# State-space rounds: a new order of ScalarE's copies, with gate products ahead of one transpose

## The chip, the cores and the metric

The kernel runs on one core of one Trainium2 chip. The metric is the device time of one execution in microseconds (us); lower is better.

## The reference

A decoder trunk of two layers over one sequence of 512 tokens with 1024 channels, in float32. Layer 0 mixes tokens with a state-space model, layer 1 with attention; each is followed by a gated convolutional feed-forward layer, and each part is modulated by a shift, a scale and a gate made from a conditioning vector (adaLN). The change touches the state-space mixer alone:

```python
def s5_mixer(h, w_in, lam_re, lam_im, log_dt, b_re, b_im, c_re, c_im, d_skip, w_glu, w_out):
    u = h @ w_in                                   # 512 x 1024
    ug = u.reshape(Bsz, S, S5_GROUPS, S5_GROUP)    # 64 groups of 16 channels
    ...                                            # each group drives 64 complex states:
    # state[t] = lam_bar * state[t-1] + B_bar u[t]; y[t] = Re(C state[t])
    y = y + d_skip * u
    y = gelu(y)
    y = y * sigmoid(y @ w_glu)
    return y @ w_out
```

## The kernel before

Matrix products are made with three TensorE products for each pair of tiles: a float32 weight is copied by ScalarE into a rounded part `w_hi`, and another engine subtracts that to get the rest, `w_lo` (`parted` and `rested` do the two steps for the input weights, `gate_hi` and `gate_lo` for the gate's, `y_hi` and `y_lo` for the mixer's output y).

The state-space mixer runs in eight rounds, m = 0 to 7, in the text "round zero" to "round seven"; each finishes one tile of 128 channels (8 groups). The 512 tokens are cut into 64 blocks of 8. Within a block the output is a direct product with a small Toeplitz table `t`; between blocks the states are scanned on VectorE. The order of instructions is the order in which the program is written, for each engine by itself (TensorE, ScalarE, VectorE, GpSimd and SyncE, whose queue SP issues nearly all transfers); nothing is rearranged by a planner. One round m does, in this order:

- `s5_scan(m)`: TensorE brings the inputs into the states (L1062); VectorE rotates, scans along the blocks with the decay table `cf` (L1073 to L1084), and leaves the states `ua`.
- the adaLN row of an earlier round is summed on VectorE (`row_sum`, L265).
- `s5_columns(m + 1)` for the next tile: TensorE makes the tile's kernel (L1007, L1010), ScalarE copies it out (`ktt`, L1015), TensorE transposes the tile's states' weights (L1021), ScalarE copies those out (`w`, L1022), TensorE transposes the kernel (L1025), ScalarE copies that out (`kt`, L1026), and SP stores it in DRAM (`s_z`).
- `s5_shifted(m + 1)`: SP loads the kernel back in shifted copies (`tw`, one buffer); in a later step ScalarE makes the table `t` of it in eight instructions (L1040).
- `inputs(m + 2)`: 24 TensorE products with the input weights of tile m + 2 (L323), a ScalarE copy `uf` (L1320), a store, and then `turn_u` loads u back in another layout.
- `s5_outputs(m)`: TensorE products with `t` (L1094) and with the states (L1103), then the gelu on ScalarE (`yg`, L1109) and a store of y.
- `parted(m + 4)` on ScalarE, `s5_decay(m + 1)` (the table `cf`, L1047), and the second step of `s5_shifted(m + 1)`, the table `t`.
- `s5_made(m + 2)` and `s5_states_out(m + 1)`: products on VectorE (L976), each followed by a sum on GpSimd (L980). The first gives `x`, which `s5_columns` reads a round later.

Beside these, one or two steps of the adaLN product of the next part run in the first four rounds (`ada_step`, L1164; `ada_load` brings the weights of the step after next, 2 x 512 KB; `row` loads one adaLN row of 512 KB), and from round four on the gate's weights are loaded and split, y is read back (`read`), and the first gate products are made (`glu_in`, L1369; `HEAD` is 4, the number of gate tiles begun early). Of the input weights `load_w(m + 4)` is issued in round m; 512 KB each.

Numbers of buffers set other waits: three `raw` buffers for loaded weights, one for `tw`, one for `cf`, one for `x`, two for `t`, and four PSUM banks (`aux`) for all small products.

Of the kernel before, what the change touches and what calls it, by code (L numbers as in the profile page):

```python
# [19 lines left out]
KT = D // P  # L20
# [796 lines left out]
class S5(Trunk):  # L817
# [301 lines left out]
    def s5(self, i, nxt):  # L1119
        nc, tc = self.nc, self.tc  # L1120
        ud = self.dram.tile([KT, GM, CG, L, B], F32, name="s5_ud")
        self.yd = self.dram.tile([KT, GM, CG, L, B], F32, name="s5_yd")
        HEAD = 4
        full = slice(0, S)
        with ExitStack() as stack:
# [16 lines left out]
            def rested(m, e=nc.gpsimd):  # L1142
                src, hi = w[m]
                lo = self.rest([P, KT, P])
                e.tensor_tensor(lo, src, hi.bitcast(F32), ALU.subtract)
                w[m] = [(hi[:, k], lo[:, k]) for k in range(KT)]
# [28 lines left out]
            with ExitStack() as start:  # L1175
# [93 lines left out]
                def turn_u(m):  # L1269
                    us[m] = self.s5q.tile([P, GM, B], F32, name="u", bufs=3)  # L1270
                    nc.sync.dma_start(us[m], ud[m].rearrange("g c j b -> (c j) g b"))
# [43 lines left out]
            def inputs(m):  # L1315
                ps = self.mm.tile([P, S], F32, name="mmp")
                for k in range(KT):
                    self.mms(ps, w[m], split_x, k, KT, full)
                uf = self.tmp.tile([P, L, B], F32, name="uf", tag="nm_t")
                nc.scalar.activation(uf, ps.rearrange("p (b j) -> p j b", j=L), AF.Copy)  # L1320
                store_u(m, uf)

            def columns_in(m):
                if m > 1 and m + 1 < KT:
                    self.s5_diagonal(m + 1)
                cols[m] = self.s5_columns(m, xs.pop(m))
                ws[m] = next(cols[m])
# [17 lines left out]
            def y_hi(*ms):  # L1345
                for m in ms:
                    nc.scalar.activation(yhi[:, m], yt[m], AF.Copy)
# [5 lines left out]
            def gate_load(n):  # L1353
                raw[n] = self.raw([P, KT, P], self.io["s5_w_glu"][n])

            def gate_hi(*ns):
                for n in ns:
                    hi[n] = self.wpool.tile([P, KT, P], F32R, name="w_hi", bufs=WB)
                    nc.scalar.activation(hi[n], raw[n], AF.Copy)

            def gate_lo(e, *ns):
                for n in ns:
                    lo[n] = self.rest([P, KT, P])
                    e.tensor_tensor(lo[n], raw[n], hi[n].bitcast(F32), ALU.subtract)
# [21 lines left out]
            for m in range(KT):  # L1386
                more, last = m + 1 < KT, m == KT - 1
                sts[m] = self.s5_scan(m, ws.pop(m), us[m], cfs.pop(m))
                next(sts[m])
                if m % 2 == 0 and m + 2 < KT:  # L1390
                    self.s5_tables(slice(m * 4 + 8, m * 4 + 16), 3, 5)
                elif m % 2 and more:
                    self.s5_tables(slice(m * 4 + 4, m * 4 + 12), 5, 6)
                if m == 0:
                    parted(3)
                if m + 3 < KT:
                    rested(m + 3)
                if m == 0:
                    turn_u(1)
                sts[m] = next(sts[m])  # L1400
                if 0 < m < KT - 3:
                    row_sum()
                if m == KT - 3:
                    read(0, 1, 2, 3)
                    gate_lo(nc.gpsimd, 0)
                if m == 0:
                    ada_step()
                    inputs(2)
                if more:
                    columns_in(m + 1)  # L1410
                    next(cols[m + 1])
                if m == KT - 3:
                    gate_hi(1)
                    gate_lo(nc.gpsimd, 1)
                if 0 < m < 4:
                    ada_step()
                if m + 4 < KT:
                    load_w(m + 4)
                if m == KT - 4:
                    for n in range(3):  # L1420
                        gate_load(n)
                if m == KT - 3:
                    gate_load(3)
                    gate_load(HEAD)
                if more:
                    ts[m + 1] = self.s5_shifted(m + 1)
                    next(ts[m + 1])
                if m and m + 2 < KT:
                    inputs(m + 2)
                if m + 2 < KT:  # L1430
                    turn_u(m + 2)
                if m < KT - 4:
                    row()
                if m == KT - 3:
                    self.rooms, self.rests = WB, 3
                    yhi = self.normed("a_hi", WHOLE)
                    ylo = self.normed("a_lo", WHOLE)
                    y_hi(0, 1, 2, 3)
                if m == KT - 2:
                    gate_hi(2)  # L1440
                    y_hi(4)
                    gate_hi(3)
                    y_hi(5)
                    for n in range(3):
                        for k in range(4):
                            glu_in(k, n, 0)
                if last:
                    y_hi(6)
                    y_lo(nc.gpsimd, 6)
                    for k in range(4):  # L1450
                        glu_in(k, 3, 0)
                    for n in range(HEAD):
                        for k in range(4):
                            glu_in(k, n, 1)
                    for n in range(HEAD):
                        for k in range(4, 6):
                            for j in range(2):
                                glu_in(k, n, j)
                outs[m] = self.s5_outputs(m, us.pop(m), ts.pop(m))
                next(outs[m])  # L1460
                outs[m].send((w2s.pop(m), sts.pop(m)))
                if m + 4 < KT:
                    parted(m + 4)
                if m == KT - 4:
                    gate_hi(0)
                if m == KT - 2:
                    gate_hi(HEAD)
                if more:
                    cfs[m + 1] = self.s5_decay(m + 1)
                    ts[m + 1] = next(ts[m + 1])  # L1470
                if steps:
                    ada_step()
                if m + 2 < KT:
                    xs[m + 2] = self.s5_made(m + 2)
                if m == KT - 3:
                    for n in range(4):
                        y_lo(nc.gpsimd, n)
                    read(4, 5)
                    row()
                    row()  # L1480
                if more:
                    w2s[m + 1] = self.s5_states_out(m + 1)
                if m == KT - 2:
                    y_lo(nc.gpsimd, 4, 5)
                    read(6)
# [378 lines left out]
```

## Time and profile before

| What | Value |
|---|---|
| Runs before | 1196.79, 1197.05, 1198.26 us (median 1197.05) |
| Profiled execution | 1199.56 us |
| Its span, first to last instruction | 1197.8 us |
| TensorE busy | 1159.5 us (97%) |
| VectorE busy | 942.5 us (79%) |
| ScalarE busy | 649.1 us (54%) |
| GpSimd busy | 204.8 us (17%) |
| Mean granted TensorE clock | 0.991 |

In the profile PE is TensorE's products, PEld its weight loads, DVE VectorE, ACT ScalarE, POOL GpSimd, and SP or SPq the queue that issues transfers. "L1025" is line 1025 of the kernel. A row of the timeline gives start, duration, engine, line, operation, what is written and read, and in brackets how long the engine stood idle before it and what ended that. The view of transfers gives the size of one and the time from its issue to its landing. The state-space rounds lie between about 50 and 180 us of the span; the text calls the engines by either name.

### The profile page before, as it was taken

Reading aid. Unit: us, or ns where it says so; the run is one execution under the profiler, and the core shown is the slowest. Engines: PE = TensorE matmul, PEld = TensorE weight load, DVE = VectorE, ACT = ScalarE, POOL = GpSimd, SP = SyncE. Lnnn points to the kernel's source line nnn. Section 1 sums busy time; section 2 is a strip of 40 time slices with the busy share of each in tenths; the row PEclk is TensorE's granted clock in tenths of the full one; section 3 lists DMA queues with packets and bytes.
Section 4 is the critical chain, followed back from the end, with each engine's and each line's share of the span. In section 5 each row is a group of like instructions: output and inputs, shape, how many; then the busy total and the mean of one; then the engine's idle time right before and its main releaser. Section 6 shows DMA issues by size and latency. Waiting matters only on the chain.

```text
span 1197.8 us, 21400 instructions
## 1 busy us (share of the span) xinstructions
PE 1159.5 (97%) x8255; PEld 1032.8 (86%) x8255; DVE 942.5 (79%) x1724; ACT 649.1 (54%) x1169; POOL 204.8 (17%) x268
## 2 busy tenths in 40 slices
PE   7987899999999999999999999999999999999997
PEld 2565788899999999989899788878999899999987
DVE  8957665879888788877676788876899878888855
ACT  3643554436666666666543576654457455555543
POOL 5664650000011111111000443330000000000000
PEclk9989899999999999999999999999999999999999
DMA  9777657833698898898704654623122332332331
GB/s 354 249 249 263 197 159 265 298 123 102 165 258 240 223 263 225 226 248 222 193 30 135 218 184 154 207 81 95 49 89 94 111 125 87 111 124 92 106 88 72
DMA packets 80006, 202.74 MB, mean 169 GB/s; under 512 B 23983, under 2 KB 26767, under 8 KB 78879
## 3 DMA queue, kind: packets, MB, share of 16 engines
q1 hardware_dynamic: 73423, 181.96, 45.2%
q0 software_dynamic: 6192, 18.88, 9.0%
q8 instruction: 65, 1.06, 0.4%
q10 hardware_dynamic: 288, 0.52, 0.1%
q14 instruction: 38, 0.31, 0.1%
HBM read 194.41 MB, written 6.92 MB: 168 GB/s over the span
## 4 chain that ended last, share of the span: by engine, by line
PE 77%; DVE 8%; DMA 7%; ACT 4%; issue 2%; POOL 1%; SPq 0%; DVEq 0%; ACTq 0%; POOLq 0%
PE mmp L323 41%; PE mmp L583 15%; PE aux L583 6%; PE mmp L1605 3%; DMA raw<-in_w_up 3%; PE aux L1751 2%; DVE w_lo L307 2%; PE aux L1734 1%; DMA raw<-in_s_w_in 1%; DVE sums L554 1%; ACT t L1040 1%; PE mmp L1369 1%; DVE ada_raw L265 1%; PE mmp L1378 1%; PE aux L1704 1%
## 5 line engine op out<-in xcount | busy, mean ns | idle before, releaser
L302 ACT ACTIVATE w_hi<-raw 128x1024 fp32r<-128x1024 f32 (+4 forms) x196 | 171.9, 887 | 114.0 <-PE mmp L323 55.1
L307 DVE TENSOR_TENSOR w_lo<-raw,w_hi 128x1024 fp32r<-128x1024 f32 (+4 forms) x153 | 154.1, 1011 | 31.6 <-ACT w_hi L302 27.8
L323 PE MATMUL mmp<-ghi,w_hi 128*128 128x512 f32 (+1 forms) x392 | 144.1, 368 | 0.0
L323 PE MATMUL mmp<-glo,w_hi 128*128 128x512 f32 (+1 forms) x392 | 143.7, 367 | 0.0
L323 PE MATMUL mmp<-ghi,w_lo 128*128 128x512 f32 (+1 forms) x392 | 143.6, 366 | 0.0
L323 PE MATMUL mmp<-a_hi,w_hi 128*128 128x256 f32 (+1 forms) x440 | 140.9, 323 | 0.0
L323 PE MATMUL mmp<-a_hi,w_lo 128*128 128x256 f32 (+1 forms) x440 | 139.0, 317 | 0.0
L323 PE MATMUL mmp<-a_lo,w_hi 128*128 128x256 f32 (+1 forms) x440 | 138.8, 316 | 0.0
L583 PE MATMUL mmp<-w_hi 128*128 128x256 f32 x420 | 116.6, 278 | 3.4 <-ACT nm_h L590 3.3
L583 PE MATMUL mmp<-w_hi,w_lo 128*128 128x256 f32 x420 | 116.0, 276 | 0.0
L583 PE MATMUL mmp<-w_lo,w_hi 128*128 128x256 f32 x420 | 116.0, 276 | 0.0
L302 ACT ACTIVATE w_hi<-sums 128x1024 fp32r<-128x1024 f32 x78 | 81.9, 1058 | 53.3 <-DVE sums L554 32.9
L307 DVE TENSOR_TENSOR w_lo<-sums,w_hi 128x1024 fp32r<-128x1024 f32 x78 | 93.9, 1217 | 2.6 <-ACT w_hi L302 2.0
L323 PEld LDWEIGHTS mmp<-a_hi,w_hi 128*128 128x128 f32 x440 | 82.2, 188 | 7.1 <-issue 2.5
L323 PEld LDWEIGHTS mmp<-a_hi,w_lo 128*128 128x128 f32 x440 | 82.6, 188 | 6.4
L265 DVE CUSTOM_DVE_ANT_0 ada_raw<-ada_raw,ada_c,rest 128x1024 f32<-128x1024 f32 x64 | 83.3, 1320 | 5.0 <-DMA ada_raw<-in_ada_rows 5.0
L323 PEld LDWEIGHTS mmp<-a_lo,w_hi 128*128 128x128 f32 x440 | 82.7, 188 | 4.6
L323 PEld LDWEIGHTS mmp<-ghi,w_lo 128*128 128x128 f32 x392 | 73.6, 188 | 12.3
L323 PEld LDWEIGHTS mmp<-ghi,w_hi 128*128 128x128 f32 x392 | 73.6, 188 | 11.2
L323 PEld LDWEIGHTS mmp<-glo,w_hi 128*128 128x128 f32 x392 | 73.6, 188 | 11.1
L583 PEld LDWEIGHTS mmp<-w_hi 128*128 128x128 f32 x420 | 78.8, 188 | 4.4 <-ACT nm_h L590 4.4
L554 DVE TENSOR_TENSOR sums<-raw 128x512 f32<-128x512 f32 x70 | 46.1, 687 | 44.8 <-DMA raw<-in_w_up 44.8
(344 smaller groups left out, 3195.5 us busy)
## 6 DMA issues: line engine op xcount, KB each, us to landing
raw<-in_w_up SPq DMA_DIRECT2D x88, 512.0 KB, 4.3
ada_raw<-in_ada_rows SPq DMA_DIRECT2D x64, 512.0 KB, 4.6
raw<-in_ada_w SPq DMA_DIRECT2D x32, 512.0 KB, 7.1
raw<-in_w_down SPq DMA_DIRECT2D x32, 384.0 KB, 4.1
raw<-in_w_down SPq DMA_DIRECT2D x32, 320.0 KB, 3.2
nf<-nfd SPq DMA_DIRECT2D x8, 1152.0 KB, 5.7
w_lo<-in_w_up POOLq DMA_DIRECT2D x17, 512.0 KB, 7.5
raw<-in_fox_qk SPq DMA_DIRECT2D x16, 512.0 KB, 3.2
```

The lines of the kernel that those rows point to most:

```text
L265: nc.vector.tensor_tensor_reduce(w, w, self.crow, 1.0, self.ada_b[:, i, m:m + 1], ALU.mult, ALU.add, self.par[i][:, m:m + 1])
L302: nc.scalar.activation(hi, src, AF.Copy)
L307: self.late = (nc.vector.tensor_tensor(lo, src, hi.bitcast(F32), ALU.subtract).ins,)
L323: self.last_mm = self.nc.tensor.matmul(o, wt, xt[:, cols], start=(k == 0 and n == 0), stop=(k == nk - 1 and n == 2),)
L554: sub = lambda o, u, v, op=ALU.subtract: nc.vector.tensor_tensor(o, u, v, op)
L583: self.last_mm = nc.tensor.matmul(o, wt[:, k], xt[:, k], start=(first and k == 0 and n == 0), stop=(k == H - 1 and n == 2), skip_group_che ...
L1040: nc.scalar.activation(t[:, :, i], tw[:, i], AF.Copy, scale=self.causal[:, i:i + 1])
L1369: nc.tensor.matmul(gps[m], hi[m][:, k], (yhi, ylo)[j][:, k], start=(k == 0 and j == 0), stop=False)
L1378: nc.tensor.matmul(gps[m], wt, xt[:, k], start=(k == 0 and part == 0 and xt is yhi), stop=(k == KT - 1 and part == 1))
L1605: self.last_mm = nc.tensor.matmul(ps[q, b][:, :n], xt[:, k, tb], wt, start=(k == 0 and i == 0), stop=(k == KT - 1 and i == 2),)
L1704: nc.tensor.matmul(ps[b][r], q[i][a, tq], kk[j][a, :N], start=(n == 0), stop=(n == 2), tile_position=(64 * r, 0), skip_group_check=True,)
L1751: nc.tensor.matmul(pv[:, c * P:], self.v[:, hp, k, r].rearrange("p t d -> p (t d)"), pp[:, r, c + 3 * k:NB + 3 * k, :].rearrange("p b t -> ...
```

## The change

The same instructions are issued, but in another order. In each round ScalarE now does `s5_columns(m + 1)` with `ktt`, `w` and `kt` first, then the table `t` of the round's own tile m (until now it was made at the end of the round before), then `cf` of the next tile, and then `parted(m + 3)` (until now `parted(m + 4)` at the end of a round); the subtraction `rested(m + 3)` follows it. In round six `t` stays ahead of the columns. On SP the load of `tw` goes ahead of `load_w` and of the gate loads, and one gate load (`HEAD`) goes behind `turn_u`. The gate pieces `gate_hi(0)` and `gate_hi(2)` go into round five and `gate_hi(3)` into round six ahead of the transpose L1025, where 16 gate products (four gate tiles, four pieces of y) now stand; until now twelve stood behind that transpose, and four in round seven.

```diff
                 if m == 0:
                     parted(3)
-                if m + 3 < KT:
-                    rested(m + 3)
-                if m == 0:
+                    rested(3)
                     turn_u(1)
                 sts[m] = next(sts[m])
...
                 if m == KT - 3:
                     read(0, 1, 2, 3)
-                    gate_lo(nc.gpsimd, 0)
...
+                if m == KT - 2:
+                    ts[m] = next(ts[m])
                 if more:
                     columns_in(m + 1)
+                if m == KT - 2:
+                    gate_hi(3)
+                    for n in range(4):
+                        for k in range(4):
+                            glu_in(k, n, 0)
+                if more:
                     next(cols[m + 1])
+                if m == KT - 3:
+                    gate_hi(0)
+                    gate_lo(nc.gpsimd, 0)
+                if m and m != KT - 2:
+                    ts[m] = next(ts[m])
                 if m == KT - 3:
                     gate_hi(1)
                     gate_lo(nc.gpsimd, 1)
+                if more:
+                    cfs[m + 1] = self.s5_decay(m + 1)
+                if m and m + 3 < KT:
+                    parted(m + 3)
+                    rested(m + 3)
                 if 0 < m < 4:
                     ada_step()
+                if more:
+                    ts[m + 1] = self.s5_shifted(m + 1)
+                    next(ts[m + 1])
                 if m + 4 < KT:
                     load_w(m + 4)
...
                 if m == KT - 3:
                     gate_load(3)
-                    gate_load(HEAD)
-                if more:
-                    ts[m + 1] = self.s5_shifted(m + 1)
-                    next(ts[m + 1])
...
                 if m + 2 < KT:
                     turn_u(m + 2)
+                if m == KT - 3:
+                    gate_load(HEAD)
...
                     y_hi(0, 1, 2, 3)
+                    gate_hi(2)
                 if m == KT - 2:
-                    gate_hi(2)
-                    y_hi(4)
-                    gate_hi(3)
-                    y_hi(5)
-                    for n in range(3):
-                        for k in range(4):
-                            glu_in(k, n, 0)
+                    y_hi(4, 5)
                 if last:
                     y_hi(6)
                     y_lo(nc.gpsimd, 6)
-                    for k in range(4):
-                        glu_in(k, 3, 0)
...
                 outs[m].send((w2s.pop(m), sts.pop(m)))
-                if m + 4 < KT:
-                    parted(m + 4)
-                if m == KT - 4:
-                    gate_hi(0)
                 if m == KT - 2:
                     gate_hi(HEAD)
-                if more:
-                    cfs[m + 1] = self.s5_decay(m + 1)
-                    ts[m + 1] = next(ts[m + 1])
```

## The prediction

> **What bounds the kernel now.** I read the page's chain first, then TensorE's waits in the stretch of the state-space rounds, then that stretch engine by engine. The chain says which engine sets the end:
>
> ```profile
> PE 77%; DVE 8%; DMA 7%; ACT 4%; issue 2%; POOL 1%; SPq 0%; DVEq 0%; ACTq 0%; POOLq 0%
> ```
>
> TensorE (PE) carries the end, so only time in which PE stands still or runs slowly can be won. The view of PE's waits from 60 to 170 us (who waited for whom, total us, times, longest) has one row:
>
> ```profile
> PE aux L1025 <- ACT ktt L1015: 16.0, 6, 4.3
> ```
>
> L1025 is the transpose that turns the next tile's kernel, and it waits in rounds one to six for ScalarE's copy at L1015. Single gaps from the timeline are 4.25, 2.61, 3.54, 1.84, 2.37 and 1.42 us. Round three shows why. The timeline (start us, us, engine, line, operation) and the chain's transfer:
>
> ```profile
> 100.15 5.91 DMA raw<-in_s_w_in
> 106.14 1.07 ACT L1139 ACTIVATE w_hi<-raw 128x1024 fp32r<-128x1024 f32 x1 [2.04 <-DMA raw<-in_s_w_in]
> 107.11 1.26 ACT L1047 ACTIVATE cf<-s_mask,s_mag 128x128 f32<-128x128 f32 x4
> 108.27 2.55 ACT L1040 ACTIVATE t<-tw,rest 128x128 f32<-128x128 f32 x8
> 110.63 0.31 ACT L1015 ACTIVATE ktt<-aux 128x128 f32<-128x128 f32 x1
> 110.84 1.04 ACT L1022 ACTIVATE w<-aux 128x512 f32<-128x512 f32 x2
> 111.78 0.26 ACT L1026 ACTIVATE kt<-aux 128x128 f32<-128x128 f32 x1
> ...
> 99.53 1.89 PE L1094 MATMUL aux<-u,t 128*128 128x64 f32 x16
> 101.36 2.00 PE L1103 MATMUL aux<-ua,w 64*128 64x63 f32 x32
> 103.29 1.06 PE L1164 MATMUL mmp<-raw,sc 128*32 128x512 f32 x8
> 104.28 1.15 PE L1062 MATMUL aux<-u,w 128*64 128x64 f32 x32
> 106.36 1.09 PE L1021 MATMUL aux<-rest,x 128*128 128x128 f32 x8
> 110.99 0.33 PE L1025 MATMUL aux<-rest,ktt 128*128 128x128 f32 x1 [3.54 <-ACT ktt L1015]
> ```
>
> Between the gelu of the old round and L1015 ScalarE does, in program order, the weights of a later tile (1.07, and it waited 2.04 for their transfer), the decay (1.26) and the tile's table t (2.55). None of these is what PE needs first. The second loss is the clock. A windows view over the stretches from L1025 to the end of the input product, rounds one to five (length, busy time of PE, PEld, DVE, ACT, POOL, then granted clock, DMA share, GB/s):
>
> ```profile
> 72.96:82.12 9.16, 9.16 (x33) 5.96 (x34) 6.67 (x8) 1.05 (x3) 5.19 (x3) 0.72 0.53 192
> 92.65:99.53 6.88, 6.88 (x33) 4.90 (x34) 4.25 (x6) 1.05 (x3) 0.00 (x0) 1.00 1.07 342
> 110.99:119.37 8.38, 8.38 (x34) 6.09 (x35) 6.67 (x8) 1.05 (x3) 2.41 (x2) 0.80 0.90 312
> 129.12:136.39 7.27, 7.27 (x26) 5.89 (x27) 7.20 (x10) 1.08 (x3) 1.65 (x1) 0.77 0.61 225
> 145.67:152.96 7.29, 7.29 (x25) 5.85 (x26) 5.93 (x7) 2.00 (x4) 4.75 (x2) 0.77 0.61 203
> ```
>
> Round two ran at clock 1.00 and took 6.88 us. Rounds one and three hold the same work and took 2.28 and 1.50 more; rounds four and five lack the adaLN step (1.00 between its starts), so 5.88 stands against 7.27 and 7.29: 1.39 and 1.41 more. Together 6.6 us.
>
> **The change, part by part.** *The main step.* ScalarE does L1015, L1022 and L1026 straight behind the gelu. From the end T of a round's output products, PE does the adaLN step (1.0), the scan's products (1.1), the columns and transposes (2.0), so L1021 ends at T+4.1. L1015 needs the columns alone, at T+3.1, takes 0.31 and lies beside the transposes (1.09). The gelu (0.66) is done by T+0.8. So the six gaps go: -16.0 us. With no hole before the input product I take the low clock to go too: -6.6 us. The most that can be won is 22.6.
>
> *The own tile's table, moved into its round.* Eight t (2.55) now follow L1026, from T+5.0 to T+7.5. The output products need them after the second adaLN step and the 24 input products, at T+10.7: hidden, with 3 us to spare; in round five, without adaLN steps, 1.6. The decay moves ahead by half a round; it waits for VectorE's scan to have read the last one, done by T+5.7, and runs to T+8.8. Then the later tile's weights (1.07) at T+8.8 to T+9.8, now half a round later than before, so that their transfer has that much longer; behind them on ScalarE stand the copy uf of the input product (due about T+10.7) and the gelu. On POOL the rest of those weights (2.4) now starts at T+9.9 and stands ahead of the sum that finishes the next x (2.4), which PE needs at T+17: ends about T+14.7, hidden.
>
> *SP's queue.* The load of tw moves ahead of the weights' load, and of the gate loads in rounds four and five; tw waits for the store z to land, and now the weights, uf's store and u's load wait behind it. The rows of SP in this stretch, then (KB each, us to landing) the transfer views for the second of the two adaLN weights, issued near 110.2, and for the row of round two:
>
> ```profile
> 91.06 0.37 SPq L1271 DMA_DIRECT2D u<-s_ud  x1
> 108.00 0.37 SPq L1271 DMA_DIRECT2D u<-s_ud  x1
> 109.56 1.12 SPq L193 DMA_DIRECT2D raw<-in_ada_w  x2
> 112.07 0.33 SPq L1027 DMA_DIRECT2D s_z<-kt  x1
> 117.26 0.33 SPq L1036 DMA_DIRECT2D tw<-s_z  x1
> 122.31 0.37 SPq L1271 DMA_DIRECT2D u<-s_ud  x1
> raw<-in_ada_w SPq DMA_DIRECT2D x1, 512.0 KB, 6.7
> ada_raw<-in_ada_rows SPq DMA_DIRECT2D x1, 512.0 KB, 4.8
> ```
>
> From u's issue the z store has landed 9.3 us later (117.26 - 108.00), and the second adaLN weight about 8.9 later (110.2 + 6.7). From u to u SP took 16.9 and 14.3 us; PE alone needs 3.8 + 1.0 + 1.1 + 2.0 + 0.3 + 1.0 + 5.6 = 14.8 a round. So the transfers, idle cover until now, become as tight as PE. I walked the rounds with these distances. u, first issued at 67.7, comes again at 85 (16.9 and half a us for z), 101 (16.0: only one pair of adaLN weights is queued behind z), 115.5 (14.5) and 130.4 (14.9, with the gate loads). PE, from its scan at 65.5 in round one, ends that round's output products at 79.3, and the next at 94.1 and 108.9 (14.8 each), 123.6 (without one adaLN step, with 0.8 of the waits below) and 137.6 (without both, with 1.2). What is late next:
>
> - The last adaLN weights, 101 + 8.9 = 109.9, against PE at 109.4, half through the step: 0.5 us.
> - x. VectorE keeps its order, and these rows set it:
>
> ```profile
> 113.25 1.29 DVE L265 CUSTOM_DVE_ANT_0 ada_raw<-ada_raw,ada_c,rest 128x1024 f32<-128x1024 f32 x1 [1.38 <-DMA ada_raw<-in_ada_rows]
> 114.46 2.35 DVE L976 TENSOR_TENSOR x<-mmp,s_bb 128x1024 f32<-128x1024 f32 x2
> 116.96 2.40 POOL L980 TENSOR_TENSOR x<-x,x 128x1024 f32<-128x1024 f32 x1 [6.43 <-DVE x L976]
> ```
>
>  The row (issued 0.4 behind u, landing 4.8) comes 5.2 after u; then 1.3 + 2.35 + 2.4 make x ready 11.25 after u: 96.3, 112.3 and 126.8. The columns want it 0.4 into themselves, at 96.6, 112.0 and 125.1: waits of 0, 0.3 and 1.7, of which I take 1.2, since the queue is shorter there.
>
> *Gate pieces and round six.* ScalarE's pieces 0 and 2 go into round five and piece 3 into round six; 16 gate products (4 of them from round seven, so no work is added) stand ahead of round six's L1025. The rows of before:
>
> ```profile
> 153.70 2.18 ACT L1347 ACTIVATE a_hi<-yt 128x512 fp32r<-128x512 f32 x4
> 162.38 0.33 SPq L1027 DMA_DIRECT2D s_z<-kt  x1
> 167.35 0.33 SPq L1036 DMA_DIRECT2D tw<-s_z  x1
> 170.96 2.58 ACT L1040 ACTIVATE t<-tw,rest 128x128 f32<-128x128 f32 x8
> ```
>
> In round five a_hi (2.18) and a piece (1.06) fill the 3.8 us of the output products, so the gelu comes at best on time; I walk it 1.9 late, which nothing on PE feels. In round six ScalarE does t first, and its tw is issued behind the y loads and z, about 138.3, landing some 3.3 later, 141.5 (at most 3.6 in the rows: 170.96 - 167.35): t to 144, L1015, L1022 to 145.3, piece 3 to 146.3. PE reaches the first of the four products with piece 3 at 143.7: a wait of 2.7. Between nothing and 4.2 us, the value with a later tw, I take 2.7. L1025 and kt then come some 5 us later against PE than before; from z to t took 167.35 - 162.38 = 5.0, then 3.6 and 2.6, and with the two row loads ahead of z on SP, t ends about 1.1 us behind its need in round seven (bounds 0 and 3). The gate load moved behind u's load is used at the end of round six: free. A hole of 2.7 us can cost the clock once, 1.4.
>
> The sum: 16.0 + 6.6 - (0.5 + 0.3 + 1.2 + 2.7 + 1.1) - 1.4 = 15.4 us. Behind the rounds nothing changes, and PE's waits between 165 and 320 us hold no row, so the gain is carried on. The profiled execution took 1199.56 (span 1197.8), which gives 1184.2; the median of the runs is 2.5 lower, which gives 1181.7.
>
> On the clock the Trainium skill has a rule ("TensorE: Matmul & The Clock Gate", section "Why this matters for your kernels"): only idle gaps over some 3 us between bursts throw PE back to half rate. By it the gaps of 4.25 and 3.54 alone would count, the clock term would be 2.28 + 1.50 = 3.8 instead of 6.6, and the time 1184.5. The trace disagrees on both sides, as these two gaps of PE and the clocks of 0.77 and 1.00 behind them show:
>
> ```profile
> 129.12 0.40 PE L1025 MATMUL aux<-rest,ktt 128*128 128x128 f32 x1 [1.84 <-ACT ktt L1015]
> 92.65 0.33 PE L1025 MATMUL aux<-rest,ktt 128*128 128x128 f32 x1 [2.61 <-ACT ktt L1015]
> ```
>
> 1.84 us sufficed in round four, and 2.61 in round two cost nothing.
>
> **The rivals.** *Nothing new is late*: 22.6 won, 1174.5. For it: u, t and the weights keep 2 us and more of margin in my walk. Against: the distances of SP above. Chance 0.13.
>
> *SP paces the rounds.* The weights no longer cover z's landing, so each turn of SP may grow by what a z by itself takes, as in round five of before:
>
> ```profile
> s_z<-kt SPq DMA_DIRECT2D x1, 64.0 KB, 2.0
> ```
>
> That is 31.2 + 4 = 35.3 over two rounds against PE's 29.6, a further loss of 5.7: 1187.4. For it: DMA shares of 0.90 and 1.07 in the windows above. Against: PE's gaps held up the same queue before. Chance 0.23.
>
> *The clock stays low.* The thin products between two input products go on for 8 us. Then 6.6 is not won: 1188.3. Against it stands the stretch with the shortest wait, which ran at full clock:
>
> ```profile
> 153.00:164.60 11.60, 10.18 (x123) 8.67 (x121) 6.41 (x10) 10.41 (x26) 7.30 (x5) 1.00 0.67 197
> ```
>
> Chance 0.07. The Trainium skill speaks for this rival (same page, section "Part 4: PE-mode transpose"): a transpose does not count as PE being busy. In the row just shown the transposes did no harm.
>
> *The gap only moves* (no change, 1197): L1025 would wait for something else as long, such as x. For it: x is ready within 1 us of its need. Chance 0.04.
>
> *Slower.* The weights of tile m+3 stand on ScalarE ahead of uf and of the gelu, and their load now waits behind tw. By my walk they land 2.5 to 4 us before ScalarE comes to them. Beyond that each us of delay shifts the gelu, L1015 and PE. Four tiles are loaded so, and to end 2.4 us slower 17.8 must be lost, 4.4 a tile: landings some 7 us later than the 5.91 above. Then 1199.5 or more. Chance 0.07.
>
> **How the numbers follow.** My forecast holds 0.46: 1181.7, its own range 1178 to 1186. The range reaches down to the first rival and up past the second and third, 1175 to 1190, leaving out the last two and the edges. A change of 0.2% (2.4 us) is about the least that can be told. Faster: 0.46 + 0.13 + 0.23 + 0.07 = 0.89; same 0.04; slower 0.07.
>
> **What would show it.** Right: L1025's wait for L1015 is gone in rounds one to five, the input products of all rounds take 5.6 to 5.9 us at clock 1.00, t ends before the output products, and PE waits in round six on piece 3 for 1 to 4 us. Wrong: PE waits of over 2 us on adaLN weights, x or u; slow input products; ScalarE idle before the weights' copy on a transfer.

## The result and the profile after

| | Before | After |
|---|---|---|
| Median of the runs on one chip | 1198.26 us (1196.79 to 1198.70) | 1191.46 us (1187.48 to 1192.38) |
| Profiled execution | 1199.56 us, span 1197.8 | 1187.48 us, span 1185.7 |
| Mean granted clock | 0.991 | 0.993 |

After is faster by 6.8 us: a ratio of 0.9941, with a 95% interval of 0.9923 to 0.9960. The forecast was 15.4 us and the range ended at 1190. The direction is right, the size less than half of what was forecast.

This is the view of PE's waits from 40 to 320 us in the changed kernel (who waited for whom, total us, times, longest). In before the same stretch has L1025 for L1015 with 16.0 us, and two small rows of 0.6 (u) and 0.3 us (L323):

```profile
PE aux L1010 <- POOL x L980: 6.1, 4, 2.9
PE mmp L1369 <- ACT w_hi L1359: 2.5, 1, 2.5
PE aux L1094 <- ACT t L1040: 1.4, 1, 1.4
PE aux L1062 <- DMA u<-s_ud: 0.9, 1, 0.9
```

L1025's wait is gone in all rounds. Three other waits stand in its place, the largest being the wait of the columns for `x`; the last row, for u, lies ahead of round one, where before waited 0.6 us too. To see what each round is worth, the windows view is cut from one round's scan (L1062) to the next, rounds one to five of before and one to six of after (length, busy time of PE, PEld, DVE, ACT, POOL, then clock, DMA share, GB/s). First before, then after:

```profile
65.54:86.87 21.33, 17.08 (x152) 12.28 (x148) 11.36 (x15) 7.16 (x20) 15.88 (x14) 0.84 0.69 225
86.87:104.28 17.41, 14.80 (x151) 11.22 (x147) 11.36 (x15) 7.16 (x20) 6.48 (x3) 1.00 0.79 264
104.28:124.11 19.83, 16.29 (x151) 12.41 (x147) 11.36 (x15) 7.34 (x21) 13.17 (x12) 0.91 0.67 224
124.11:140.14 16.03, 14.19 (x136) 12.05 (x132) 11.26 (x15) 6.69 (x19) 8.56 (x6) 0.89 0.62 215
140.14:156.71 16.57, 14.20 (x133) 12.01 (x131) 10.06 (x13) 10.06 (x25) 11.96 (x8) 0.90 0.67 215
```

```profile
65.57:80.30 14.73, 14.73 (x151) 11.33 (x148) 9.73 (x12) 7.24 (x20) 8.09 (x6) 1.00 0.84 286
80.30:97.18 16.88, 14.61 (x150) 11.20 (x148) 14.28 (x18) 7.23 (x20) 10.32 (x10) 1.00 0.84 284
97.18:113.63 16.45, 15.69 (x151) 11.33 (x148) 11.77 (x16) 7.24 (x20) 10.88 (x7) 1.00 0.69 225
113.63:126.28 12.65, 12.43 (x133) 10.86 (x132) 8.80 (x14) 7.17 (x19) 9.57 (x9) 1.00 0.67 198
126.28:143.15 16.87, 14.00 (x134) 12.20 (x132) 14.13 (x17) 10.60 (x25) 14.75 (x8) 0.90 0.77 242
143.15:158.04 14.89, 12.40 (x125) 10.54 (x123) 8.29 (x11) 9.00 (x23) 11.16 (x8) 0.89 0.71 226
```

Rounds one to four of after ran at full clock. Round one lost nothing; rounds two and three stand above 14.6 us of products by the waits for x and a slow adaLN step; rounds five and six have waits and a clock of 0.90 and 0.89. Round six also holds four gate products that stood in round seven before.

From round one's scan to the first product behind round seven (the gate product of L1378) the profiled execution of before took 65.54 to 181.30, 115.8 us, and that of after 65.57 to 171.95, 106.4: 9.4 us won. The rest of the span took 1082.0 and 1079.3. This part lies between 1078.4 and 1082.0 us in the profiled executions of all kernels here, and so the table of the experiments gives the two parts for each kernel.

### The profile page after: what moved, and what is told of

Same layout as the page of the kernel before. It is cut to its first block, busy times and chain, and to the rows that moved or that the text cites. A ratio compares the mean times of both kernels' runs of the same rounds, so it can differ in the third digit from the quotient of the medians.

```text
span 1185.7 us, 21406 instructions
## 1 busy us (share of the span) xinstructions
PE 1156.9 (98%) x8255; PEld 1031.8 (87%) x8255; DVE 944.6 (80%) x1724; ACT 651.1 (55%) x1169; POOL 201.2 (17%) x268
## 3 DMA queue, kind: packets, MB, share of 16 engines
q8 instruction: 65, 1.06, 0.4%
## 4 chain that ended last, share of the span: by engine, by line
PE 83%; DMA 7%; DVE 5%; issue 2%; ACT 1%; POOL 1%; SPq 0%; DVEq 0%; ACTq 0%; POOLq 0%
PE mmp L323 43%; PE mmp L583 18%; PE aux L583 7%; PE mmp L1607 3%; DMA raw<-in_w_up 2%; PE aux L1753 2%; PE aux L1736 1%; DMA ada_raw<-in_ada_rows 1%; DMA s_ud<-uf 1%; PE aux L1706 1%; PE mmp L1378 1%; PE mmp L1190 1%; PE mmp L1235 1%; DVE x L976 1%; DVE w_lo L307 1%
## 5 line engine op out<-in xcount | busy, mean ns | idle before, releaser
L323 PE MATMUL mmp<-ghi,w_hi 128*128 128x512 f32 (+1 forms) x392 | 144.2, 368 | 0.0
L323 PE MATMUL mmp<-glo,w_hi 128*128 128x512 f32 (+1 forms) x392 | 143.7, 367 | 0.0
L323 PE MATMUL mmp<-ghi,w_lo 128*128 128x512 f32 (+1 forms) x392 | 143.6, 366 | 0.0
L323 PE MATMUL mmp<-a_hi,w_hi 128*128 128x256 f32 (+1 forms) x440 | 140.9, 322 | 0.0
L323 PE MATMUL mmp<-a_hi,w_lo 128*128 128x256 f32 (+1 forms) x440 | 139.0, 317 | 0.0
L323 PE MATMUL mmp<-a_lo,w_hi 128*128 128x256 f32 (+1 forms) x440 | 138.8, 316 | 0.0
L265 DVE CUSTOM_DVE_ANT_0 ada_raw<-ada_raw,ada_c,rest 128x1024 f32<-128x1024 f32 x64 | 87.3, 1382 | 15.0 <-DMA ada_raw<-in_ada_rows 15.0
L323 PEld LDWEIGHTS mmp<-a_hi,w_hi 128*128 128x128 f32 x440 | 82.2, 188 | 7.1 <-issue 2.6
L323 PEld LDWEIGHTS mmp<-a_hi,w_lo 128*128 128x128 f32 x440 | 82.6, 188 | 6.4
L323 PEld LDWEIGHTS mmp<-a_lo,w_hi 128*128 128x128 f32 x440 | 82.7, 188 | 4.6
L323 PEld LDWEIGHTS mmp<-ghi,w_lo 128*128 128x128 f32 x392 | 73.6, 188 | 12.3
L323 PEld LDWEIGHTS mmp<-ghi,w_hi 128*128 128x128 f32 x392 | 73.6, 188 | 11.2
L323 PEld LDWEIGHTS mmp<-glo,w_hi 128*128 128x128 f32 x392 | 73.6, 188 | 11.1
L583 PEld LDWEIGHTS mmp<-w_lo,w_hi 128*128 128x128 f32 x420 | 78.8, 188 | 0.0
```

Of the source, the lines that this page charges most:

```text
L265: nc.vector.tensor_tensor_reduce(w, w, self.crow, 1.0, self.ada_b[:, i, m:m + 1], ALU.mult, ALU.add, self.par[i][:, m:m + 1])
L323: self.last_mm = self.nc.tensor.matmul(o, wt, xt[:, cols], start=(k == 0 and n == 0), stop=(k == nk - 1 and n == 2),)
L583: self.last_mm = nc.tensor.matmul(o, wt[:, k], xt[:, k], start=(first and k == 0 and n == 0), stop=(k == H - 1 and n == 2), skip_group_che ...
```

## The experiments

Each kernel of the table is the changed kernel with the edit told below; each ratio is to before on the same chip. "Rounds" is the stretch just described in the profiled execution, "rest" the span without it. The profiled execution is one of the runs and need not stand for the median: after, x_first and tail_y were profiled at the lower end of their ranges, again, tail and tail_w at the upper end. What an edit is worth is therefore read from the medians and intervals, and what waits for what from the traces.

| Run | Median us (range) | Ratio, 95% interval | Rounds | Rest |
|---|---|---|---|---|
| again | 1191.60 (1186.5 to 1193.3) | 0.9955 (0.9935 to 0.9975) | 113.0 | 1078.5 |
| x_first | 1192.52 (1188.55 to 1194.03) | 0.9970 (0.9952 to 0.9989) | 106.1 | 1080.7 |
| sp_old | 1186.97 (1180.6 to 1191.0) | 0.9922 (0.9886 to 0.9958) | 105.1 | 1078.5 |
| gate_old | 1188.23 (1183.39 to 1191.41) | 0.9933 (0.9911 to 0.9954) | 106.4 | 1078.8 |
| combo | 1184.26 (1181.45 to 1185.95) | 0.9886 (0.9867 to 0.9906) | 103.7 | 1078.8 |
| tail | 1181.75 (1179.8 to 1185.88) | 0.9873 (0.9851 to 0.9894) | 104.4 | 1079.7 |
| tail_w | 1182.37 (1180.27 to 1183.99) | 0.9872 (0.9854 to 0.9891) | 103.1 | 1079.1 |
| rest_late | 1187.31 (1183.77 to 1194.29) | 0.9920 (0.9897 to 0.9944) | 106.6 | 1078.4 |
| tail_y | 1179.75 (1178.4 to 1184.64) | 0.9859 (0.9835 to 0.9884) | 95.6 | 1081.0 |

**again: the changed kernel as it is.**

> The changed kernel once more, for a second trace of it. Theory: the state-space rounds repeat to half a microsecond (scan of round seven 10 us earlier than before, as in the first trace), and the 4 us between its executions (1187.5 to 1192.4) arise behind the rounds, in the feed-forward layer. Rival: they arise in the rounds, where waits of PE decide whether the clock falls, 1.4 us at a time. Time 1188 to 1192 on both.

The median came out as before, 1191.6. This profiled execution took 1193.3, and it is nearer to the median than the first one, which was the fastest of its runs. Its rest is as short as any other's (1078.5); its rounds took 113.0 us, 6.6 more than in the first execution. So what these two executions differ by arises in the rounds, and not behind them as the theory had it: the rival was right. PE's rows that waited longest:

```profile
84.20 0.64 PE L1010 MATMUL aux<-x,s_cd 128*32 128x128 f32 x16 [2.21 <-POOL x L980]
114.11 3.14 PE L1164 MATMUL mmp<-raw,sc 128*32 128x512 f32 x8 [2.48 <-DMA raw<-in_ada_w]
133.98 0.98 PE L1010 MATMUL aux<-x,s_cd 128*32 128x128 f32 x16 [2.85 <-POOL x L980]
155.38 2.07 PE L1369 MATMUL mmp<-a_hi,w_hi 128*128 128x512 f32 x4 [3.03 <-ACT w_hi L1359]
```

and the windows of its rounds three, five, six and seven (the last up to the first gate product):

```profile
97.24:117.18 19.94, 16.75 (x151) 11.42 (x147) 13.26 (x17) 7.23 (x20) 14.21 (x8) 0.91 0.63 201
129.56:146.43 16.87, 14.02 (x134) 12.21 (x132) 14.11 (x17) 10.21 (x25) 14.75 (x8) 0.90 0.78 242
146.43:164.51 18.08, 15.05 (x126) 13.10 (x124) 8.32 (x11) 9.29 (x23) 12.46 (x9) 0.73 0.69 217
164.51:178.42 13.91, 13.91 (x115) 12.16 (x113) 11.62 (x15) 4.83 (x12) 1.98 (x6) 0.86 0.33 83
```

The adaLN weights came late here: one store of y held SP for 2.09 us (0.42 in the first execution), and the weights behind it were issued at 106.86 instead of 104.73. Behind the wait of 3.03 in round six the clock was 0.73, against 0.89 in the first execution. Of the 6.6 us, 3.5 lie in round three, where the store stood (19.94 against 16.45), and 3.2 in round six (18.08 against 14.89); rounds four and five took within 0.3 us what they took in the first execution. So 2 us on one queue became 3.5 on PE in the same round. That they also caused the loss in round six is not shown.

**x_first: x is made ahead of the row sum.** The row sum goes from behind the scan to the end of the round.

```diff
-                if 0 < m < KT - 3:
-                    row_sum()
...
                     w2s[m + 1] = self.s5_states_out(m + 1)
+                if 0 < m < KT - 3:
+                    row_sum()
```

> VectorE makes x and w ahead of the adaLN row's sum, which moves to the end of the round. Theory A: x came late because VectorE stands in the row's sum, first for the row's transfer and then for GpSimd's subtraction beside it; so PE's four waits for x (6.1 us) fall under 1 us and the time falls by 4 to 6 us against the changed kernel, to about 1186. Rival B: SP's queue paces the rounds; the waits come back at the adaLN weights, u or t, and less than 2 us is won.

The waits for x went, and rounds one to five took 14.53, 14.54, 15.76, 12.35 and 12.78 us at clock 1.00. The scan of round six began at 134.35, where before began it at 156.71: 22.4 us earlier, and 21.2 of it since the scan of round one (64.39 against 65.54). That is all that the prediction said could be won up to there, 16.0 + 6.6 without the 1.42 of round six. But the median did not move (1192.52 against again's 1191.60 on the same chip): the rival came true, that SP paces the rounds. Rounds six and seven (up to the gate product), in windows, and the rows of PE that waited:

```profile
134.35:152.51 18.16, 13.14 (x123) 10.98 (x123) 10.15 (x11) 10.65 (x25) 12.44 (x7) 0.81 0.69 215
152.51:170.46 17.95, 15.31 (x115) 13.39 (x113) 11.35 (x16) 5.35 (x14) 4.15 (x8) 0.83 0.41 134
```

```profile
139.00 0.79 PE L1007 MATMUL aux<-dd,rest 128*128 128x128 f32 x2 [3.50 <-DMA dd<-in_s_dd]
147.61 1.20 PE L1369 MATMUL mmp<-a_hi,w_hi 128*128 128x512 f32 x4 [1.52 <-ACT w_hi L1359]
163.79 3.13 PE L1094 MATMUL aux<-u,t 128*128 128x64 f32 x16 [2.64 <-ACT t L1040]
```

The waits lead to SP, whose queue holds in order the gate loads, u's store and load, the reads of y, the diagonal dd, the stores z and the loads tw:

```profile
121.70 1.33 SPq L193 DMA_DIRECT2D raw<-in_s_w_glu  x3
123.12 0.48 SPq L1267 DMA_DIRECT2D s_ud<-uf  x1
131.19 0.38 SPq L1271 DMA_DIRECT2D u<-s_ud  x1
...
134.81 0.43 SPq L999 DMA_DIRECT2D dd<-in_s_dd  x1
135.29 0.43 SPq L1027 DMA_DIRECT2D s_z<-kt  x1
139.20 0.32 SPq L1036 DMA_DIRECT2D tw<-s_z  x1
```

Three gate loads of 512 KB stand ahead of u's store, u's load waits for that store, and it could be issued only 8.07 us later (131.19 - 123.12), where the same step took 5.1 to 5.6 us in the turns before and after it. y's reads, dd, z and tw stand behind it in the queue. PE had got ahead of its transfers: of the 21.2 us this execution kept 9.7 (115.8 - 106.1), and the other 11.5 went within two rounds, in waits of 8.0 us together (0.30 for u and the three rows above) and in the low clock.

**sp_old: SP's old order.** The load of `tw` goes behind the weights' and the gate loads again; all else as in the change.

```diff
-                if more:
-                    ts[m + 1] = self.s5_shifted(m + 1)
-                    next(ts[m + 1])
                 if m + 4 < KT:
                     load_w(m + 4)
...
+                if more:
+                    ts[m + 1] = self.s5_shifted(m + 1)
+                    next(ts[m + 1])
```

> The changed kernel with SP's old order alone: the loads of the input weights and of gate tiles 0 to 3 ahead of the load of tw. Theory A: a turn of SP is shorter by up to 2 us, since these loads fill the time in which z lands; the rows and with them x come earlier, 1 to 3 us faster than the changed kernel. Rival C: t comes late instead and PE waits at L1094, 1 us or more slower.

1186.97, some 4.6 us under again; the two intervals overlap, so this alone shows little. The rival's wait came as well: PE stood 3.2 us for t in round seven (L1094). The same edit made on top of x_first tells more:

**combo: x_first and SP's old order together.**

> The changed kernel with x made ahead of the row's sum and with SP's old order of the weights' and gate loads. Theory A: x's waits are gone, as they were with the first edit alone, and the stages up to the scan of round six end near 135 us; what remains is the line of transfers in rounds five to seven, which the old order shortens by 2 to 3 us: 1183 to 1187. Rival B: the two edits win the same time, and it comes out like the better of the two, 1187.

1184.26. The ratio of 0.9886 (0.9867 to 0.9906) against x_first's 0.9970 (0.9952 to 0.9989), each to before beside it, is 0.84 points lower: some 10 us, from SP's order alone (the changed kernel's own ratio came out 0.14 points apart on two chips). So the load of tw ahead of the others costs time rather than winning it, once PE is no longer held by x. In x_first the queue stood from z (116.81) to tw (121.28) with nothing to issue. In combo z was issued at 116.64, and the gate loads filled the time:

```profile
117.48 4.09 SPq L193 DMA_DIRECT2D raw<-in_s_w_glu  x3
121.66 0.38 SPq L1036 DMA_DIRECT2D tw<-s_z  x1
```

u's load then came 6.37 us behind its store (128.51 - 122.14) instead of 8.07. Not all was won: round six of combo held a wait of 3.3 us for a gate piece, at a clock of 0.78. Whether x costs time once SP is in order is less sure: 0.9922 with x late (sp_old) stands against 0.9886, some 4 us, with intervals that overlap.

**gate_old: the gate products back behind L1025.** Twelve in round six behind that transpose, four in round seven, piece 3 and t behind kt, as before the change.

> The changed kernel with the gate products of rounds six and seven as before: twelve behind the transpose L1025, four in round seven, piece 3 and table t behind kt. Theory A: the wait of 2.5 us for piece 3 goes, but round seven's t is bound by SP (y's second read, two rows and z stand in line), so PE waits there as much longer: within 1.5 us of the changed kernel. Rival D: the gate part costs its waits of 2.5 and 1.4 and 1.4 of clock, and 4 to 5 us are won.

1188.23 against again's 1191.60, with intervals that overlap, and the profiled rounds took 106.4 us, to a tenth what after's took. A gate piece was waited for in round seven instead (2.1 us). Putting the gate products ahead of the transpose bought nothing that can be measured; whether it cost something, as the rival has it, these runs leave open.

**rest_late: GpSimd's subtraction behind its sum for x.**

```diff
                     parted(m + 3)
-                    rested(m + 3)
...
                     xs[m + 2] = self.s5_made(m + 2)
+                if m and m + 3 < KT:
+                    rested(m + 3)
```

The load of the next weights and that of gate tile 2 go behind it.

> The changed kernel with x still behind the row's sum, but GpSimd's subtraction for the later tile behind its sum for x (and that tile's next load, with gate tile 2, behind it, at the end of the round). Theory A, the lock: with no GpSimd work beside it the row's sum takes 1.3 us in all four rounds, where it took up to 3.2, and PE's waits for x fall from 6.1 to 2 or 3 us, what the row's landing explains: 3 us faster than the changed kernel. Rival E: the sum is long because its transfer lands in parts; it stays at 2.6 to 3.2 us.

This is the test of why x was late. In the changed kernel, VectorE's row sum (L265) and GpSimd's subtraction (L1145), rounds one to four:

```profile
76.11 3.20 DVE L265 CUSTOM_DVE_ANT_0 ada_raw<-ada_raw,ada_c,rest 128x1024 f32<-128x1024 f32 x1 [3.52 <-DMA ada_raw<-in_ada_rows]
91.90 2.74 DVE L265 CUSTOM_DVE_ANT_0 ada_raw<-ada_raw,ada_c,rest 128x1024 f32<-128x1024 f32 x1 [2.32 <-DMA ada_raw<-in_ada_rows]
109.30 1.28 DVE L265 CUSTOM_DVE_ANT_0 ada_raw<-ada_raw,ada_c,rest 128x1024 f32<-128x1024 f32 x1 [4.40 <-DMA ada_raw<-in_ada_rows]
124.42 1.49 DVE L265 CUSTOM_DVE_ANT_0 ada_raw<-ada_raw,ada_c,rest 128x1024 f32<-128x1024 f32 x1 [3.58 <-DMA ada_raw<-in_ada_rows]
75.89 2.35 POOL L1145 TENSOR_TENSOR w_lo<-raw,w_hi 128x1024 fp32r<-128x1024 f32 x1 [4.50 <-DMA s_yd<-yg]
91.18 2.37 POOL L1145 TENSOR_TENSOR w_lo<-raw,w_hi 128x1024 fp32r<-128x1024 f32 x1 [1.38 <-ACT w_hi L1139]
106.52 2.37 POOL L1145 TENSOR_TENSOR w_lo<-raw,w_hi 128x1024 fp32r<-128x1024 f32 x1 [1.38 <-ACT w_hi L1139]
122.47 2.35 POOL L1145 TENSOR_TENSOR w_lo<-raw,w_hi 128x1024 fp32r<-128x1024 f32 x1 [1.39 <-ACT w_hi L1139]
```

Where the sum starts inside a subtraction it ends 1.07 to 1.09 us behind the subtraction's end (79.31 - 78.24, 94.64 - 93.55, 125.91 - 124.82); where it starts 0.41 us behind that end (109.30 - 108.89) it takes 1.28. So the sum does not run beside GpSimd's instruction, it waits for it. In rest_late nothing runs on GpSimd at that place, and the four sums took 1.28 each; its first and its last:

```profile
75.84 1.28 DVE L265 CUSTOM_DVE_ANT_0 ada_raw<-ada_raw,ada_c,rest 128x1024 f32<-128x1024 f32 x1 [3.30 <-DMA ada_raw<-in_ada_rows]
...
123.48 1.28 DVE L265 CUSTOM_DVE_ANT_0 ada_raw<-ada_raw,ada_c,rest 128x1024 f32<-128x1024 f32 x1 [3.29 <-DMA ada_raw<-in_ada_rows]
```

In round one the row landed as late as in after, 6.7 us behind its issue (75.84 - 69.10), and yet the wait for x that follows in round two fell from 2.27 to 0.24 us. So most of that wait was the stretched sum, and not the row. All waits for x together fell from 6.1 to 3.5 us. Of these 2.5 are in round five, where VectorE still waits 3.29 us for the row. The median is 1187.31, its interval overlapping again's, and the profiled rounds took 106.6 us, as long as after's: a new wait of 3.9 us, of L1021 for VectorE's `ua`, stands in round six.

**tail and tail_w: the transfers sorted by who needs them first.** On top of x_first: gate tiles 0 and 1 are loaded ahead of tw in round four and tile 2 behind u's load, the reads of y behind z in round five, and two adaLN rows behind the last tw instead of ahead of z. In tail_w the load of the input weights goes ahead of tw as well.

```diff
-                if m == KT - 3:
-                    read(0, 1, 2, 3)
...
                 if m == KT - 3:
+                    read(0, 1, 2, 3)
                     gate_hi(0)
...
+                if m == KT - 4:
+                    gate_load(0)
+                    gate_load(1)
                 if more:
                     ts[m + 1] = self.s5_shifted(m + 1)
                     next(ts[m + 1])
+                if m == KT - 2:
+                    row()
+                    row()
...
                     turn_u(m + 2)
+                if m == KT - 4:
+                    gate_load(2)
```

> x ahead of the row's sum, and SP's line in rounds four to six shortened: gate tile 2 is loaded behind u's load, gate tiles 0 and 1 ahead of tw, y's first reads behind the store z, the two adaLN rows of round five behind the last tw. Theory A: the gain of 22 us that the first edit showed at round six's scan was given back in these transfers alone; PE's waits in rounds six and seven (7.6 us there) fall by 4 to 6 us: 1183 to 1186. Rival B: the waits move to piece 3 or the last t, under 2 us won: 1189 or more.

> The kernel with the shortened line of transfers, and the input weights' load ahead of tw too. Theory A: as without that, or up to 2 us faster, since a turn of SP is shorter in rounds one to three: 1181 to 1185. Rival: t is late instead, 1 to 3 us slower.

1181.75 and 1182.37: the waits for dd, t and piece 3 are gone in both, those for the adaLN weights remain (2.7 and 1.5 us), and between the two nothing can be told. A new wait of 4.3 us stands in round six of both, here in tail_w:

```profile
144.11 1.94 PE L1021 MATMUL aux<-rest,x 128*128 128x128 f32 x8 [4.29 <-DVE ua L1084]
```

The likely reading is that the transposes have been given the PSUM bank that the scan of the same round uses until VectorE has written ua, and otherwise have the bank that the gelu of round five frees: in gate_old and combo L1021 waits for that gelu (L1109, 0.7 and 0.3 us). The profile leaves buffer numbers out, so the banks themselves are not shown. If it is so, the order of the copies around the gelu can change which bank they get. It is not the only thing that does: rest_late has the wait with the gelu where the change has it.

**tail_y: tail_w with the gelu of round five ahead of the copies of y.**

```diff
                 if m == KT - 3:
...
-                    y_hi(0, 1, 2, 3)
                     gate_hi(2)
...
                 outs[m].send((w2s.pop(m), sts.pop(m)))
+                if m == KT - 3:
+                    y_hi(0, 1, 2, 3)
```

> As tail_w, with ScalarE's copies of y tiles 0 to 3 (a_hi, 2.6 us) behind the gelu of round five instead of ahead of it. Theory: the wait of 4.3 us at L1021 in round six comes from the order of releases: with the gelu late, the transposes are given the bank of the scan of the same round, and wait for VectorE's ua. With the gelu ahead the transposes have the gelu's bank: the 4.3 us go, and the first gate products wait instead for a_hi and piece 3, 1 to 2 us together; round six takes 15 to 16 us instead of 18.2, and the time falls by 2 to 3 us against tail_w, to about 1179.5. Rival: ScalarE's copies between the gelu and piece 3 (about 9 us) set round six in either order: L1369 then waits about 4 us in L1021's place and the time stays within 1 us of tail_w's.

1179.75, the best here: 0.9859 (0.9835 to 0.9884) of before. The wait at L1021 is gone, and L1369 waits 1.2 us and not 4, as the rival had it. PE's waits in it, and the windows of rounds five, six and seven (the last up to the gate product):

```profile
PE aux L1010 <- POOL x L980: 1.5, 2, 1.3
PE mmp L1369 <- ACT w_hi L1359: 1.2, 1, 1.2
```

```profile
121.58:135.31 13.73, 12.47 (x134) 10.86 (x132) 10.63 (x15) 9.07 (x22) 13.65 (x8) 1.00 0.87 262
135.31:147.63 12.32, 10.89 (x126) 9.23 (x124) 9.85 (x11) 9.29 (x24) 9.96 (x7) 1.00 0.72 225
147.63:159.87 12.24, 12.24 (x114) 10.74 (x112) 10.77 (x15) 5.36 (x13) 5.05 (x5) 1.00 0.55 173
```

Round six took 12.32 us instead of tail_w's 18.24 (136.95 to 155.19). That is more than the wait of 4.3: the clock stayed at 1.00, where it was 0.81 over this round in tail_w. The forecast of 15 to 16 us for the round was too cautious by this. In the medians the gain over tail_w, 2.6 us, is within what either varies by, so the removed wait is shown and its worth is not.

## Why the prediction was wrong, step by step

Full-clock rounds without waits take 14.54 us with adaLN steps (x_first), 12.38 without, 11.16 in round six (tail_y's 12.32 less 1.16) and 12.24 in round seven: 91.8 us for the stretch that took 115.8 in before. So 24.0 us could be won, not 22.6; the low clock also touched products that I had not counted. Of this the first execution of after won 9.4 and again 2.8 (115.8 - 113.0); the 6.8 us between the medians lie between these two. Where the remainder stayed, term by term:

| Step of the prediction | Forecast | after | again |
|---|---|---|---|
| L1025's six waits end | 16.0 won | won | won |
| x | 1.5 lost | 6.1 | 5.8 |
| last adaLN weights | 0.5 | 1.1 (step of 2.15 against 1.06) | 2.5 |
| piece 3 in round six | 2.7 | 2.5 | 3.0 |
| t of round seven | 1.1 | 1.4 | none |
| low clock | 1.4, once | 3.0 | 9.6 |

The last row is PE's busy time above that of the same round at full clock: 14.00 - 12.47 and 12.40 - 10.89 in after; 16.75 - 14.54, 14.02 - 12.47, 15.05 - 10.89 and 13.91 - 12.24 in again (in its round three 2.1 of the 2.2 lie in the adaLN step, 3.14 us against 1.06, over which the clock was 0.53). The columns make 14.1 and 20.9, of the 14.6 and 21.2 that the stretch lies above 91.8.

**Right.** ScalarE's order was what held L1025, and with kt first the wait is gone. Full clock came back with it in every round that had no new wait in it or in the round before it: rounds one to five of x_first ran at 1.00 and won the 21.2 us that the prediction had for them. t of the own tile is hidden in rounds one to five. Piece 3 and round seven's t cost about what was forecast in after, but partly by luck, since both sides of these races ran later than in my walk: piece 3 came at 151.5 instead of 146.3, and PE stood ready for it at 149.1 instead of 143.7.

Three steps failed: x and the low clock were priced too small, and SP's turns were longer than walked.

**Wrong: x.** The step "1.3 + 2.35 + 2.4 make x ready 11.25 after u" took the row sum at its old 1.3, and it called GpSimd's subtraction hidden, since the sum behind it ends at T+14.7 and PE wants x at T+17. It is hidden from PE, but not from VectorE: moved to this place it holds the row sum for 1.9 us in round one and 1.5 in round two. My walk also began with the second x; the first, with a row that landed 6.7 us after its issue (69.43 to 76.11) instead of 4.8, was waited for 2.27 us, half of the 4.6 that x cost more than forecast. In round five the sum took only 0.2 more, and the wait of 2.87 (I had 1.7, and took 1.2) is the turn of u and the landing of the row. x's term was too small, but it is not by itself why the time fell short: with x's waits gone and SP's order unchanged (x_first) the median stayed where it was.

**Wrong: the clock.** "A hole of 2.7 us can cost the clock once" priced one hole. All nine waits of 3.03 to 4.30 us in these rounds of all kernels were followed by a low clock, 0.72 to 0.81 over the stretch or round behind them. A shorter hole may cost it or not. What it cost was 1.5 us (round five of after) to 4.2 (round six of again). Two rounds five show this, with a wait of the same length at the same place; again had 0.90 in the row above, gate_old 1.00:

```profile
129.53 0.64 PE L1010 MATMUL aux<-x,s_cd 128*32 128x128 f32 x16 [2.88 <-POOL x L980]
```

```profile
125.09:140.39 15.30, 12.43 (x134) 10.86 (x132) 14.13 (x17) 8.10 (x21) 13.18 (x8) 1.00 0.75 244
```

In sp_old and rest_late the wait at this place was 2.85 and 2.46 us, and the clock of the round 0.90 in both. So below 3 us the length of a hole does not decide alone; what else does is not settled by these runs. A new wait of 2.5 to 3 us came to between its own length (gate_old) and more than twice that (round six of again: 3.03 of wait and 4.2 of clock). The prediction also said that its trace disagreed "on both sides" with the rule of over 3 us; only one side did: the 1.84 us with 0.77 behind it speak against the rule, but the 2.61 us that cost nothing are what it gives.

**Wrong: SP.** I had the turns of u at 16.0, 14.5 and 14.9 us; after's were 16.3, 15.7 and 16.0 (86.87, 103.17, 118.83 and 134.85). PE's own rounds were longer too, so these turns alone do not show who held whom; combo against x_first does, for the kernel with x out of the way. The rival "SP paces the rounds" at 1187.4 was nearer than the forecast, and its reason is seen in the traces: z's landing is no longer covered. In after's rounds five to seven z and tw are issued as follows:

```profile
138.63 0.43 SPq L1027 DMA_DIRECT2D s_z<-kt  x1
143.17 0.32 SPq L1036 DMA_DIRECT2D tw<-s_z  x1
156.30 0.42 SPq L1027 DMA_DIRECT2D s_z<-kt  x1
161.15 0.33 SPq L1036 DMA_DIRECT2D tw<-s_z  x1
```

From z to tw the queue stands for 4.5 and 4.9 us, and the loads behind tw, which wait for nothing, stand with it. Landing itself took longer as well, by the median of the eight rounds: z 4.5 us against 2.7 in before, tw 4.1 against 3.3. My walk put the turn of u at the landing of z and half a us, and left out that the weights, u's store and y's reads then follow behind tw one by one. In combo and tail a part of these loads goes out while z lands.

The other rivals: the weights of tile m+3 were not late (ScalarE stood idle before none of the copies of rounds two to four in after); the gap did not merely move; the transposes do no harm to the clock, since rounds full of them ran at 1.00. What the experiments leave open is what besides a wait lowers the clock, how much of sp_old's 4.6 us belongs to which load, and why one store held SP for 2.09 us in again.

## What to carry to other kernels

When a wait goes that held the whole loop, list what each other queue does during the time that it took, since that time was their cover: here SP's landing of z, the adaLN row and one GpSimd instruction lived in it. Give a queue that must wait for a store something to issue ahead of that wait, and let loads that nobody needs soon stand behind the ones that the next round needs. An instruction moved on an idle engine can still stretch one on a busy engine, so compare the durations at its new place too, and not only who waits for its end.

## What was unexpected of the hardware

VectorE's row sum and GpSimd's subtraction exclude each other: 1.28 us alone, 1.49 to 3.20 when it starts within one, ending some 1.08 us behind it each time. The nine traces that have such a case agree: wherever a sum started more than 0.2 us before the end of a running GpSimd instruction, it ended 1.07 to 1.09 us behind that end. It holds the other way too. In x_first the sum (75.84, 3.24 us) started within GpSimd's sum for x, and GpSimd's next one started while it ran:

```profile
75.64 2.35 POOL L980 TENSOR_TENSOR x<-x,x 128x1024 f32<-128x1024 f32 x1
77.94 3.36 POOL L980 TENSOR_TENSOR w<-w,x 128x1024 f32<-128x1024 f32 x1
```

3.36 us instead of 2.37: it was held until VectorE's sum ended at 79.08. The Trainium skill states this ("SBUF — State Buffer", section "Who interferes with whom"): a VectorE instruction with two inputs in SBUF contends with a GpSimd instruction that reads SBUF, and whichever starts first holds the shared ports to its end. The traces agree with it in both directions. The prediction put the stretch of the sums at nothing; in rounds one and two of after it was 1.9 and 1.5 us.

Below 3 us the clock did not follow the length of the wait ahead of it: 2.88 us at 1.00 in gate_old, 2.87 and 2.85 at 0.90 in after and again, at the same instruction. The rule of over some 3 us, cited in the prediction ("TensorE: Matmul & The Clock Gate" of the Trainium skill, section "Why this matters for your kernels"), again does not separate these: by it none of the three would have cost anything, and two did. The nine waits of over 3 us, each with a low clock behind it, agree with it.
